# Narrower weights for the low parts of the probabilities in the value products of attention, and another order of their matmuls

## The chip, the cores and the metric

The kernel runs on one core of one Trainium2 chip. The metric is device time in microseconds (us), the median of several runs. Engines are named as the profile names them: PE (TensorE, matmuls) with PEld (its weight loads), DVE (VectorE), ACT (ScalarE), POOL (GpSimd), SP (SyncE, which issues most DMAs).

## The reference

Two layers of a decoder trunk over 1024 tokens of 1024 features, in float32. Each layer has a mixer, two attention branches that run in parallel, and a gated convolutional feed-forward block. What the change touches is the last step of attention, probabilities times values:

```python
p = jnp.exp(scores - mx)                                    # dilated windows, softmax
o = jnp.einsum('brhnqk,brhnkc->brhnqc', p, vw) / den
...
attn = jnp.where(causal, jnp.exp(log_sigmoid(z) + later), 0.0)  # stick-breaking
return jnp.einsum('bhqk,bhkc->bhqc', attn, vt)
```

There are 4 stick-breaking heads, which see all earlier keys, and 12 dilated-window heads in three groups: one near group (each query sees the last 128 keys) and two far groups with dilations 4 and 16. A head has 64 features.

## The kernel before, in words

**Split numbers.** PE takes its operands as fp32r, which holds fewer bits than float32. So an operand x is kept as two parts, hi = x rounded to fp32r (ACT, line 145) and lo = x - hi (DVE, line 153), and a product is a sum of hi x hi, hi x lo and lo x hi. The dense projections spell that out as three matmuls of 512 moving columns (lines 1063 to 1065, and `product`, lines 187 to 189).

**The value product.** Values lie in tiles of 128 keys by 128 columns: columns 0 to 63 are the high half of the head's 64 features, 64 to 127 the low half. Such a tile is the stationary operand (the weight) of a matmul. The moving operand is a block of probabilities, transposed by PE so that keys lie on the partitions, and split by `parts` (line 651) into a high tile and a low tile. Each block of values meets both tiles in two matmuls, which add into one PSUM bank `o`: partitions 0 to 63 collect the products with the high half, 64 to 127 those with the low half. `fold` (line 658) adds the two halves when the bank is complete. So before the change four products are summed: hi x hi, hi x lo, lo x hi and lo x lo.

**Units.** One call of `apply` is called a unit here. Its matmuls have 256 or 128 moving columns, 128 where a block of keys meets only one of two query blocks:

- `stick_item`, `apply` (line 754; profile line 763): one item for each head and each pair of query blocks, 16 items a layer; in each item units for kb = 2qp, 2qp-2, ..., 0, two key blocks each. In the first unit of an item the second key block has 128 columns; otherwise all have 256.
- `near_item`, `apply` (line 822; profile line 830): 4 items a layer, each with five units by the list of `sets` at line 851, for example `[(2, [2, 3]), (3, [3])]`, a pair of 256 columns and a pair of 128; the last unit is `[(7, [7])]` alone.
- `far_item`, `apply` (line 931; profile lines 936 and 938): 16 items a layer, each with two units (one for each far group), of 256 and of 128 columns.

**The order around it.** PE's instruction order is the order of the program. `attend` (line 374) interleaves, in small steps, an item's turns (transposes of probabilities, then `parts`) and its applies, each apply after the next turn, with the scores of the next item. After each such step `dense.advance(rate)` puts in steps of the dense projections for later items: RATE (1.03 to 1.32) for the stick-breaking items, RATE_N (0.75) for near and RATE_T (0.58) for far. With a rate under 1, some steps have no dense work behind them, and then a unit is followed by the next transposes or scores. DMAs for later items are issued from `fetch` by counts of such steps. DVE, ACT and the queues get their order from a planner that knows priorities (`high_priority`) and orders set by hand (`add_manual_dep`).

Of the kernel before, what the change touches and what calls it, by code (L numbers as in the profile page):

```python
# [16 lines left out]
P = 128  # L17
# [23 lines left out]
IN_ORDER = {ET.PE, ET.Activation, ET.DVE, ET.Pool}  # L41
HEAD = 4
SECOND = 0.35
RATE = (1.03, 1.17, 1.27, 1.32)
RATE_N = 0.75
RATE_T = 0.58
# [18 lines left out]
def trunk_kernel(ctx, tc, x, norm1, w_in, b_gate, w_br, w_o, norm2, w_up, conv_w, conv_b, w_down, norm_f, out, depth=None, probe=None):  # L65
    nc = tc.nc
    act, dve, pe, pool = nc.scalar, nc.vector, nc.tensor, nc.gpsimd
# [64 lines left out]
    def small(name, dtype=F32):  # L132
        return sb.tile([P, 512], dtype, tag="pt", bufs=PT, name=name)
# [517 lines left out]
    def parts(src, n, name):  # L651
# [3 lines left out]
            split(hi[:, :n], lo[:, :n], src[:, :n], "is")  # L655
        return hi, lo

    def fold(dst, o):

        n = o.shape[-1]  # L660
        tmp = small("fold")
        with tc.high_priority(offset=AHEAD):
            act.copy(tmp[0:64, :n], o[64:128, :])
            dve.tensor_tensor(dst, o[0:64, :], tmp[0:64, :n], ALU.add)
# [33 lines left out]
    def stick_item(dense, u, qp):  # L698
        q, k, v = R["slots"][:, qp], R["kv"][:, 0, :], R["kv"][:, 1, :]
        pr, s = divmod(u, 2)  # L700
        rows, st, shared, left = {}, {}, {}, []

        def score(a):
            L = P * (2 * qp + a + 1)
            bt = rows[a] = sb.tile([P, T], F32, tag="p4", bufs=4, name="beta")
            if a == 0:
                st[0] = sb.tile([P, 2, T], F32, tag="xa", bufs=4, name="stay")
            sv = st[0][:, a, :]
            for c1 in range(L, 0, -512):
                c0 = max(0, c1 - 512)  # L710
                w = c1 - c0
                z = bank("s", "z")
                scores(z[:, :w], *(q[:, x, a * P : a * P + P] for x in range(2)), k[:, c0:c1])
                with tc.high_priority(offset=AHEAD):
                    act.activation(bt[:, c0:c1], z[:, :w], AF.Sigmoid)
                    last = act.activation(sv[:, c0:c1], z[:, :w], AF.Sigmoid, scale=-1.0)
                    if (u, qp, a, c0) == (3, 0, 1, 0):
                        one = table(AF.Exp, zero[:, 0:1])
                        tc.add_manual_dep(one.ins, last.ins.name, NO_SYNC, reason="behind")
                    if c1 == L:  # L720
                        pool.affine_select(bt[:, L - P : L], bt[:, L - P : L], [[-1, P]], ALU.is_gt, 0.0, base=0, channel_multiplier=1)
                (SCANS if c1 == L else left).append((shared, bt, sv, c0, c1, L))
            if a:
                SCANS.extend(left)
                dense.rows += 1
                scans(2)

        def scans(most):

            while SCANS and most:  # L730
                most -= 1
                _, bt, sv, c0, c1, L = SCANS.pop(0)
                rev = sv[:, c0:c1][:, ::-1]
                if c1 == L:
                    one = dve.tensor_tensor_scan(rev, rev, over[:, HF - (c1 - c0) : HF][:, ::-1], 1.0, ALU.mult, ALU.max)
                else:
                    one = dve.tensor_tensor_scan(rev, rev, zero[:, 0:1].to_broadcast([P, c1 - c0]), sv[:, c1 : c1 + 1], ALU.mult, ALU.add)
                if "dve" in LAST:
                    tc.add_manual_dep(one.ins, LAST["dve"], NO_SYNC, reason="in turn")
                k0, k1 = max(0, c0 - 1), c1 - 1  # L740
                with tc.high_priority(offset=AHEAD):
                    LAST["mult"] = dve.tensor_tensor(bt[:, k0:k1], bt[:, k0:k1], sv[:, k0 + 1 : k1 + 1], ALU.mult).ins.name

        def turn(kb):
            while any(x[0] is shared and x[4] > kb * P for x in SCANS):
                scans(1)
            tp = bank("t", "sb_t")
            todo = [(j, a) for j in range(2) for a in range(2) if kb + j <= 2 * qp + a]
            for c, (j, a) in enumerate(todo):
                pe.transpose(tp[:, c * P : c * P + P], rows[a][:, (kb + j) * P : (kb + j + 1) * P], ident)  # L750
            shared[kb] = parts(tp, len(todo) * P, "sb")
            scans(2)

        def apply(kb):
            first = kb == 2 * qp
            if first:
                shared["o"] = bank("o", "sb_o")[:, :256]
                dense.free[qp] = u + 1
            o = shared["o"]
            for j in range(2):  # L760
                c = P if first and j else 0
                for p in (0, 1):
                    pe.matmul(
                        o[:, c:256],
                        v[:, (kb + j) * P : (kb + j + 1) * P],
                        shared[kb][p][:, 256 * j : 256 * j + 256 - c],
                        start=(first and j == 0 and p == 0),
                        stop=(kb == 0 and j == 1 and p == 1),
                        skip_group_check=True,
                    )  # L770
            if kb == 0:
                out_ = small("ob")[0:64, 0:256]
                fold(out_, o)
                nc.sync.dma_start(obd[64 * s : 64 * s + 64, pr, qp * 256 : (qp + 1) * 256], out_)

        sc = [lambda: score(0), lambda: score(1)]
        return sc, [(lambda kb=kb: turn(kb), lambda kb=kb: apply(kb)) for kb in range(2 * qp, -2, -2)]


    def near_item(dense, pr, s):  # L780
# [6 lines left out]
        k, v = kv[:, 0, :], kv[:, 1, :]  # L787
        got, shared = {}, {}
# [33 lines left out]
        def apply(i, some, n, first, last):  # L822
            if first:
                shared["o"] = bank("o", "o0")
            o = shared["o"]
            w = 0
            for kb, bs in some:
                c0, nb = (bs[0] - 4 * n) * P, len(bs) * P
                for p in (0, 1):
                    pe.matmul(  # L830
                        o[:, c0 : c0 + nb],
                        v[:, kb * P : (kb + 1) * P],
                        shared[i][p][:, w * P : w * P + nb],
                        start=(first and w == 0 and p == 0),
                        stop=(last and kb == some[-1][0] and p == 1),
                        skip_group_check=True,
                    )
                w += len(bs)
            if last:
                fold(on[64 * s : 64 * s + 64, pr, n * HF : (n + 1) * HF], o)  # L840
                if s == 1 and n == 1:
                    tp = bank("o", "st0_t")
                    pe.transpose(tp[0:32, 0:P], st.rearrange("p a s b -> p (a s b)"), ident)
                    row = sb.tile([32, P], F32, tag="pt", bufs=PT, name="st0_r")
                    with tc.high_priority(offset=AHEAD):
                        act.copy(row, tp[0:32, 0:P])
                    nc.sync.dma_start(dn[pr].rearrange("c (b p) -> (c b) p", p=P), row)
# [37 lines left out]
    def far_item(dense, pr, s, r, share):  # L885
        i = 8 * pr + 4 * s + r
# [5 lines left out]
        shared = {}  # L892
# [38 lines left out]
        def apply(g):  # L931
            if r % 2 == 0 and g == 0:
                share["o"] = bank("o", "o1")
            o, oc, vt = share["o"], 256 * (r % 2), R["v", i][:, g]
            for p in (0, 1):
                pe.matmul(o[:, oc : oc + 256], vt[:, 0:P], shared[g][p][:, 0:256], start=(r % 2 == 0 and g == 0 and p == 0), stop=False, skip_group_check=True)
            for p in (0, 1):
                pe.matmul(o[:, oc + P : oc + 256], vt[:, P:256], shared[g][p][:, 256:384], start=False, stop=(r % 2 == 1 and g == 1 and p == 1), skip_group_check=True)
            if g == 1:
                dense.applied = i + 1  # L940
            if r % 2 == 1 and g == 1:
                if R["ot", pr] is None:
                    R["ot", pr] = sb.tile([P, T], F32, tag="ot", name="ot")
                fold(R["ot", pr][64 * s : 64 * s + 64, 512 * (r // 2) : 512 * (r // 2) + 512], o)
                if s == 1 and r == 3:
                    join(dense, pr)
# [389 lines left out]
    def mixer(l, pending):  # L1336
# [43 lines left out]
        for j in range(16):  # L1380
            items.append((f"B{j}", [f"FB{j // 4 * 4 + 3}"], [], RATE[3 - j % 4], lambda j=j: stick_item(dense, j // 4, 3 - j % 4)))
        for v in range(4):
# [530 lines left out]
    def enter(l):  # L1913


        def go(rest, last):
# [9 lines left out]

            drive(norm(0, g1[:, 0, :], "t", raw=True), second(), SECOND, 3)
            x_move(1, True)
# [304 lines left out]
```

## Time and profile before

| | |
|---|---|
| time, median of 3 runs | 2612.03 us (2611.89 to 2614.1) |
| span of the profiled execution (its own time) | 2610.5 us |
| PE matmuls busy | 2600.8 us, 12647 instructions |
| PE weight loads | 2178.5 us, 12647 instructions |
| DVE busy | 2085.6 us |
| ACT busy | 1349.7 us |
| mean granted clock of PE | 1.000 |

The span goes from the first to the last instruction of one profiled execution. A timeline row gives the start, the duration (both in us), the engine, the line, the operation, the tiles it writes and reads, and shapes: `128*128` is the weight, the next pair the moving operand (partitions by columns), or, for a load, the weight. Rows of groups end with the count, the busy time in us and the mean of one in ns. Durations of matmuls are modelled and overlap each other, since matmuls are pipelined; starts are recorded. A weight load is shown as an instruction of its own (PEld).

### The profile page before, as it was taken

How to read it: one execution, taken by the hardware profiler on the slowest of the kernel's cores; microseconds unless marked ns; L12 is line 12 of the kernel's file. 1: busy time of each engine (PE TensorE's matmuls, PEld its weight loads, DVE VectorE, ACT ScalarE, POOL GpSimd, SP SyncE). 2: the span in 40 equal slices, each digit the busy share in tenths (PEclk: the TensorE clock that was granted, in tenths of full speed). 3: DMA queues.
4: the chain of work that ended last, by engine and by line, in shares of the span. 5: the costliest groups of instructions: out<-in, count | busy, mean ns of one | idle time of the engine just before them, and what ended most of it. 6: DMA issues, size and time to landing. Idle time of an engine off the chain costs nothing.

```text
span 2610.5 us, 36058 instructions
## 1 busy us (share of the span) xinstructions
PE 2600.8 (100%) x12647; PEld 2178.5 (83%) x12647; DVE 2085.6 (80%) x3485; ACT 1349.7 (52%) x2521; POOL 105.5 (4%) x145
## 2 busy tenths in 40 slices
PE   9999999999999999999999999999999999999999
PEld 8888888888888888888888888888888888888887
DVE  8877777795988888897677788777869888889965
ACT  6555666574554555422445555656645555544225
POOL 3000000030000000000000000000300000000000
PEclk9999999999999999999999999999999999999999
DMA  7433578873244444688344436788633344446963
GB/s 255 151 120 130 163 208 214 236 245 97 90 145 156 142 167 140 235 328 316 145 143 148 127 129 183 196 231 234 208 100 122 122 163 144 150 165 261 344 239 119
DMA packets 401409, 470.60 MB, mean 180 GB/s; under 512 B 24500, under 2 KB 315980, under 8 KB 399436
## 3 DMA queue, kind: packets, MB, share of 16 engines
q1 hardware_dynamic: 400364, 465.90, 55.2%
q0 software_dynamic: 704, 2.13, 0.4%
q8 instruction: 100, 1.64, 0.3%
q14 instruction: 81, 0.66, 0.1%
q10 hardware_dynamic: 160, 0.27, 0.0%
HBM read 305.59 MB, written 162.63 MB: 179 GB/s over the span
## 4 chain that ended last, share of the span: by engine, by line
PE 98%; DVE 1%; ACT 1%; DMA 0%; issue 0%; POOL 0%; DVEq 0%; ACTq 0%; POOLq 0%
PE u_a L1064 6%; PE u_a L1063 6%; PE u_a L1065 6%; PE d_ps L1827 5%; PE d_ps L1828 5%; PE d_ps L1829 5%; PE i_a L1063 5%; PE i_a L1065 5%; PE i_a L1064 5%; PE u_c L1063 3%; PE u_c L1064 3%; PE u_c L1065 3%; PE i_c L1063 3%; PE i_c L1065 3%; PE i_c L1064 3%; PE o_ps L187 2%
## 5 line engine op out<-in xcount | busy, mean ns | idle before, releaser
L145 ACT CAST w_hi<-up_a 128x512 fp32r<-128x512 f32 x280 | 173.9, 622 | 276.8 <-DVE up_a L1681 120.5
L153 DVE TENSOR_TENSOR w_lo<-up_a,w_hi 128x512 fp32r<-128x512 f32 x280 | 189.4, 688 | 83.5 <-ACT w_hi L145 83.5
L145 ACT CAST w_hi<-in_a 128x512 fp32r<-128x512 f32 x252 | 156.2, 622 | 164.7 <-PE i_c L1064 38.5
L153 DVE TENSOR_TENSOR w_lo<-in_a,w_hi 128x512 fp32r<-128x512 f32 x252 | 172.9, 688 | 73.8 <-ACT w_hi L145 65.7
L1838 DVE TENSOR_TENSOR x<-x,d_ps 128x512 f32<-128x512 f32 x220 | 150.1, 684 | 60.3 <-PE d_ps L1829 57.0
L1064 PE MATMUL u_a<-t_lo,w_hi 128*128 128x512 f32 x320 | 124.6, 389 | 0.0
L1063 PE MATMUL u_a<-t_hi,w_hi 128*128 128x512 f32 x320 | 124.6, 389 | 0.0
L1065 PE MATMUL u_a<-hh,w_lo 128*128 128x512 f32 x320 | 124.5, 389 | 0.0
L1064 PE MATMUL u_a<-hl,w_hi 128*128 128x512 f32 x320 | 124.5, 389 | 0.0
L1065 PE MATMUL u_a<-t_hi,w_lo 128*128 128x512 f32 x320 | 124.5, 389 | 0.0
L1063 PE MATMUL u_a<-hh,w_hi 128*128 128x512 f32 x320 | 124.5, 389 | 0.0
L1827 PE MATMUL d_ps<-gd_in,w_hi 128*128 128x512 f32 x316 | 123.3, 390 | 0.0
L1828 PE MATMUL d_ps<-gd_in,w_hi 128*128 128x512 f32 x316 | 123.1, 389 | 0.0
L1829 PE MATMUL d_ps<-gd_in,w_lo 128*128 128x512 f32 x316 | 123.0, 389 | 0.0
L1063 PE MATMUL i_a<-hh,w_hi 128*128 128x512 f32 x288 | 119.2, 414 | 0.0
L1063 PE MATMUL i_a<-t_hi,w_hi 128*128 128x512 f32 x288 | 118.3, 411 | 0.0
L1065 PE MATMUL i_a<-hh,w_lo 128*128 128x512 f32 x288 | 113.2, 393 | 0.0
L1065 PE MATMUL i_a<-t_hi,w_lo 128*128 128x512 f32 x288 | 113.1, 393 | 0.0
L1064 PE MATMUL i_a<-t_lo,w_hi 128*128 128x512 f32 x288 | 113.0, 392 | 0.0
L1064 PE MATMUL i_a<-hl,w_hi 128*128 128x512 f32 x288 | 112.8, 392 | 0.0
L1827 PE MATMUL d_ps<-gd_in,wd 128*128 128x512 f32 x284 | 111.1, 391 | 0.0
L1829 PE MATMUL d_ps<-gd_in,wd 128*128 128x512 f32 x284 | 110.6, 389 | 0.0
(409 smaller groups left out, 7830.6 us busy)
## 6 DMA issues: line engine op xcount, KB each, us to landing
gd<-g SPq DMA_DIRECT2D x154, 512.0 KB, 3.3
gd_in<-gd SPq DMA_DIRECT2D x154, 512.0 KB, 6.3
up_a<-in_w_up_dram SPq DMA_DIRECT2D x80, 512.0 KB, 5.6
in_a<-in_w_in_dram SPq DMA_DIRECT2D x72, 512.0 KB, 5.5
wd_raw<-in_w_down_dram SPq DMA_DIRECT2D x22, 1024.0 KB, 11.4
gin<-gs SPq DMA_DIRECT2D x32, 512.0 KB, 4.2
w_raw<-in_w_o_dram SPq DMA_DIRECT2D x64, 256.0 KB, 2.8
gs<-u SPq DMA_DIRECT2D x48, 256.0 KB, 2.6
```

The source lines that it names most:

```text
L145: one = act.copy(hi, src)
L153: two = dve.tensor_tensor(lo, src, f32(hi), ALU.subtract)
L187: pe.matmul(o, lh, rh, start=(first and i == 0), stop=False, skip_group_check=share)
L1063: pe.matmul(o, w[0][:, c], rh, start=(first and i == 0), stop=False, skip_group_check=True)
L1064: pe.matmul(o, w[0][:, c], rl, start=False, stop=False, skip_group_check=True)
L1065: pe.matmul(o, w[1][:, c], rh, start=False, stop=(last and i == 3), skip_group_check=True)
L1827: pe.matmul(o, wh[:, c], gh, start=(i == 0 and k in (0, 4, 5)), stop=False, skip_group_check=True)
L1828: pe.matmul(o, wh[:, c], gl, start=False, stop=False, skip_group_check=True)
L1829: pe.matmul(o, wl[:, c], gh, start=False, stop=(i == m - 1), skip_group_check=True)
L1838: dve.tensor_tensor(x, x, o, ALU.add)
```

## The change

A new function `values_on` takes a unit's list of (values, columns of `o`, columns of the probabilities). It first multiplies the high probabilities with all 128 columns of each value block, widest block first. Then it goes through the blocks in the opposite order and multiplies the low probabilities with only the first 66 columns of the values, which write partitions 0 to 65 of `o`. So lo x hi stays, and lo x lo goes, but for the first two of its 64 features. The three `apply` functions call it in place of their own loops; the number of matmuls is the same.

```diff
+LOW = 66
...
+    def values_on(o, todo, part_, first, last):
+
+        todo = sorted(todo, key=lambda x: x[1].start - x[1].stop)
+        for i, (vals, to, at) in enumerate(todo):
+            pe.matmul(o[:, to], vals, part_[0][:, at], start=(first and i == 0), stop=False, skip_group_check=True)
+        for i, (vals, to, at) in reversed(list(enumerate(todo))):
+            pe.matmul(o[0:LOW, to], vals[:, 0:LOW], part_[1][:, at], start=False, stop=(last and i == 0), skip_group_check=True)
...
@@ stick_item, apply @@
-            for j in range(2):
-                c = P if first and j else 0
-                for p in (0, 1):
-                    pe.matmul(
-                        o[:, c:256],
-                        v[:, (kb + j) * P : (kb + j + 1) * P],
-                        shared[kb][p][:, 256 * j : 256 * j + 256 - c],
...
+            values_on(
+                o,
+                [(v[:, (kb + j) * P : (kb + j + 1) * P], slice(P if first and j else 0, 256), slice(256 * j, 256 * j + (P if first and j else 256))) for j in range(2)],
+                shared[kb],
+                first,
+                kb == 0,
+            )
@@ near_item, apply @@
-            w = 0
+            w, todo = 0, []
             for kb, bs in some:
                 c0, nb = (bs[0] - 4 * n) * P, len(bs) * P
-                for p in (0, 1):
-                    pe.matmul(
-                        o[:, c0 : c0 + nb],
-                        v[:, kb * P : (kb + 1) * P],
-                        shared[i][p][:, w * P : w * P + nb],
...
+                todo.append((v[:, kb * P : (kb + 1) * P], slice(c0, c0 + nb), slice(w * P, w * P + nb)))
                 w += len(bs)
+            values_on(o, todo, shared[i], first, last)
@@ far_item, apply @@
-            for p in (0, 1):
-                pe.matmul(o[:, oc : oc + 256], vt[:, 0:P], shared[g][p][:, 0:256], ...)
-            for p in (0, 1):
-                pe.matmul(o[:, oc + P : oc + 256], vt[:, P:256], shared[g][p][:, 256:384], ...)
+            todo = [(vt[:, 0:P], slice(oc, oc + 256), slice(0, 256)), (vt[:, P:256], slice(oc + P, oc + 256), slice(256, 384))]
+            values_on(o, todo, shared[g], r % 2 == 0 and g == 0, r % 2 == 1 and g == 1)
```

More of the change, by code (lines that the diff above doesn't have):

```diff
@@ L759, in apply @@
             o = shared["o"]
-            for j in range(2):
-                c = P if first and j else 0
-                for p in (0, 1):
-                    pe.matmul(
-                        o[:, c:256],
-                        v[:, (kb + j) * P : (kb + j + 1) * P],
-                        shared[kb][p][:, 256 * j : 256 * j + 256 - c],
[L767 to L770, printed above, removed]
+            values_on(
[5 more added lines that the diff above has]
+            )
             if kb == 0:
@@ L825, in apply @@
             o = shared["o"]
-            w = 0
+            w, todo = 0, []
             for kb, bs in some:
                 c0, nb = (bs[0] - 4 * n) * P, len(bs) * P
-                for p in (0, 1):
-                    pe.matmul(
-                        o[:, c0 : c0 + nb],
-                        v[:, kb * P : (kb + 1) * P],
-                        shared[i][p][:, w * P : w * P + nb],
[L834 to L837, printed above, removed]
+                todo.append((v[:, kb * P : (kb + 1) * P], slice(c0, c0 + nb), slice(w * P, w * P + nb)))
                 w += len(bs)
+            values_on(o, todo, shared[i], first, last)
             if last:
@@ L934, in apply @@
             o, oc, vt = share["o"], 256 * (r % 2), R["v", i][:, g]
-            for p in (0, 1):
-                pe.matmul(o[:, oc : oc + 256], vt[:, 0:P], shared[g][p][:, 0:256], start=(r % 2 == 0 and g == 0 and p == 0), stop=False, skip_group_check=True)
-            for p in (0, 1):
-                pe.matmul(o[:, oc + P : oc + 256], vt[:, P:256], shared[g][p][:, 256:384], start=False, stop=(r % 2 == 1 and g == 1 and p == 1), skip_group_check=True)
+            todo = [(vt[:, 0:P], slice(oc, oc + 256), slice(0, 256)), (vt[:, P:256], slice(oc + P, oc + 256), slice(256, 384))]
+            values_on(o, todo, shared[g], r % 2 == 0 and g == 0, r % 2 == 1 and g == 1)
             if g == 1:
```

## The prediction

> **What bounds the kernel now.** I read the head of the page, its chain of waits, a table by stretches, the timeline of TensorE around the changed matmuls, the groups by shape, and last the waits.
>
> ```profile
> span 2610.5 us, 36058 instructions
> ...
> PE 2600.8 (100%) x12647; PEld 2178.5 (83%) x12647; DVE 2085.6 (80%) x3485; ACT 1349.7 (52%) x2521; POOL 105.5 (4%) x145
> ...
> PE 98%; DVE 1%; ACT 1%; DMA 0%; issue 0%; POOL 0%; DVEq 0%; ACTq 0%; POOLq 0%
> ```
>
> TensorE is busy for the whole span and is 98% of the chain that ended last. So what an edit of its stream is worth is read from start to start inside that stream: a matmul's shown duration has a pipelined tail in it, and "busy" hides a matmul that waits for its weights. Three shapes matter: a 512-wide matmul of the projections, and the 256-wide and 128-wide matmuls of the value products ("wide" and "narrow" from here; every weight load before has 128 columns). The timeline of one value product of the stick-breaking branch, TensorE's matmuls, then its weight loads:
>
> ```profile
> 90.73 0.28 PE L763 MATMUL sb_o<-sbh,kv 128*128 128x256 f32 x1
> 90.84 0.28 PE L763 MATMUL sb_o<-sbl,kv 128*128 128x256 f32 x1
> 90.96 0.22 PE L763 MATMUL sb_o<-sbh,kv 128*128 128x128 f32 x1
> 91.02 0.28 PE L763 MATMUL sb_o<-sbl,kv 128*128 128x128 f32 x1
> 91.13 0.45 PE L1063 MATMUL i_a<-hh,w_hi 128*128 128x512 f32 x1
> 91.42 0.39 PE L1064 MATMUL i_a<-hl,w_hi 128*128 128x512 f32 x1
> 91.65 0.39 PE L1065 MATMUL i_a<-hh,w_lo 128*128 128x512 f32 x1
> ```
>
> ```profile
> 90.96 0.19 PEld L763 LDWEIGHTS sb_o<-sbl,kv 128*128 128x128 f32 x1
> 91.07 0.19 PEld L1063 LDWEIGHTS i_a<-hh,w_hi 128*128 128x128 f32 x1
> ```
>
> Each load starts when the matmul before it has started, and runs beside it. A 512-wide matmul takes 0.23 us from start to start (91.42 to 91.65), a wide one 0.11 to 0.12, a narrow one 0.06 (90.96 to 91.02). Loads follow each other every 0.11 us (90.96, 91.07). So a load hides behind a 512-wide matmul, just hides behind a wide one, and does not hide behind a narrow one: half of it sticks out. The narrow low product lasts 0.28 where the narrow high one lasts 0.22, and the next 512-wide one 0.45 where the usual is 0.39. These are the two places where a load sticks out, one behind each narrow matmul.
>
> **What a load costs by its columns.** Eight matmuls of one moving column show the pace of loads alone, and two groups of transposes have loads of 32 and of 128 columns:
>
> ```profile
> 673.13 0.97 PEld L538 LDWEIGHTS nrm_t<-ones,nrm 128*128 128x128 f32 x8 [0.35 <-issue]
> ```
>
> ```profile
> L763 PEld LDWEIGHTS sb_o<-sbl,kv 128*128 128x128 f32 x160 | 30.3, 190 | 3.2
> L1034 PEld LDWEIGHTS j_ps<-ident,fx 128*128 128x128 f32 x32 | 3.7, 141 | 0.5
> L843 PEld LDWEIGHTS st_t<-ident,st 128*32 128x32 f32 x4 | 0.4, 94 | 0.0
> ```
>
> (0.97 - 0.19)/7 = 0.111 us a load, so of the 0.19 shown some 0.078 is a latency that the next load doesn't wait for. Take the same latency from the loads of transposes: 141 - 78 = 63 ns for 128 columns and 94 - 78 = 16 ns for 32, or 0.49 and 0.50 ns a column. The pace is proportional to the columns there, with nothing fixed. If the loads of the values behave so, 66 columns take 111 x 66/128 = 57 ns, and show as some 78 + 57 = 135 ns. The bounds: 111 ns (columns don't matter) and 111 - 62 x 0.49 = 81 ns (the columns count only as in a transpose). I take 57, because the two transposes leave no fixed part; 81 and 111 are rivals below.
>
> **The change part by part.** No instruction is added or removed: 360 high and 360 low products stay. The lows load 66 columns instead of 128, and the order of a unit goes from high, low, high, low to high wide, high narrow, low narrow, low wide.
>
> ```profile
> L763 PE MATMUL sb_o<-sbl,kv 128*128 128x256 f32 x128 | 34.1, 283 | 0.0
> L936 PE MATMUL o<-p1l,slots 128*128 128x256 f32 x64 | 18.7, 292 | 0.3 <-DVE p1l L153 0.2
> L938 PE MATMUL o<-p1l,slots 128*128 128x128 f32 x64 | 17.7, 277 | 0.0
> L938 PE MATMUL o<-p1h,slots 128*128 128x128 f32 x64 | 14.3, 223 | 0.0
> L830 PE MATMUL o<-p0l,kv 128*128 128x256 f32 x48 | 13.2, 289 | 0.0
> L763 PE MATMUL sb_o<-sbl,kv 128*128 128x128 f32 x32 | 8.9, 279 | 0.0
> L763 PE MATMUL sb_o<-sbh,kv 128*128 128x128 f32 x32 | 7.2, 224 | 0.0
> L830 PE MATMUL o<-p0l,kv 128*128 128x128 f32 x24 | 6.6, 277 | 0.0
> L830 PE MATMUL o<-p0h,kv 128*128 128x128 f32 x24 | 5.3, 222 | 0.0
> ```
>
> Narrow lows: 32 + 64 + 24 = 120. Eight of them stand alone (the last key block of each of the 8 near items, [(7,[7])]); 112 share a unit with a wide pair. Wide lows: 128 + 64 + 48 = 240; less 112 leaves 128, that is 64 units of two wide pairs.
>
> First exposure, the narrow low waiting for its own load. In the new order that load has 57 ns and runs behind the narrow high (60 ns): hidden. The price is the difference of the low and the high group: 279 - 224 = 55, 277 - 223 = 54, 277 - 222 = 55. So 32 x 55 + 64 x 54 + 24 x 55 = **6.5 us**.
>
> Second exposure, what follows the narrow low. Now a load of 66 columns (the low wide's) lies behind the narrow low, and the full load of whatever follows the unit lies behind the low wide, which covers it as 90.73 to 90.96 do. Before a 512-wide matmul the price is 0.06 (0.45 against 0.39); I take 55 ns, as for the first. Before a transpose it is smaller:
>
> ```profile
> 442.44 0.30 PE L926 MATMUL t<-ident,p 128*128 128x128 f32 x1
> 442.57 0.27 PE L927 MATMUL t<-ident,p 128*128 128x128 f32 x1
> ...
> 1814.97 0.29 PE L926 MATMUL t<-ident,p 128*128 128x128 f32 x1
> ```
>
> 0.02 to 0.03, taken as 25 ns. In the timeline 32 of the 112 units are followed by transposes (the far ones between these two rows); the other 80 by a dense matmul or, where the narrow pair came first, by their own wide pair at 0.05. So 80 x 55 + 32 x 25 = **5.2 us**. The eight lone ones keep this exposure, since their low is followed by the dense stream as before.
>
> Units of two wide pairs:
>
> ```profile
> 96.00 0.28 PE L763 MATMUL sb_o<-sbh,kv 128*128 128x256 f32 x1
> 96.11 0.28 PE L763 MATMUL sb_o<-sbl,kv 128*128 128x256 f32 x1
> 96.23 0.40 PE L1063 MATMUL i_a<-t_hi,w_hi 128*128 128x512 f32 x1
> ```
>
> 0.12 a matmul where 0.11 is the least (90.73 to 90.84): two of the four loads shrink, at 5 ns each, 64 x 10 ns = **0.6 us**; bounds 0 and 64 x 20 = 1.3.
>
> The order itself. The low of a unit waits for VectorE's subtraction, and a high no longer stands behind it:
>
> ```profile
> 422.73 0.28 PE L936 MATMUL o<-p1h,slots 128*128 128x256 f32 x1
> 423.08 0.38 PE L936 MATMUL o<-p1l,slots 128*128 128x256 f32 x1
> ...
> PEld o L936 <- DVE p1l L153: 1.7, 5, 0.4
> ```
>
> Here the low starts 0.35 after the high instead of 0.12. Five such waits, 1.7 us together, could lose at most the narrow high that now fills them, 5 x 0.06 = 0.3 us, and half a load each. I book 0; at the other end, with waits that grow as TensorE comes earlier, I allow -1 us. The queues of SyncE, ScalarE and GpSimd get the same instructions; the fold still waits for the unit's last matmul, which comes earlier.
>
> Sum: 6.5 + 5.2 + 0.6 = 12.3 us. The profiled span of 2610.5 becomes 2598.2. The median shown, 2612.03, lies 1.5 above that span, and what lies around the span does not change: **2599.7 us**.
>
> What must keep up is the far stage, where units are densest:
>
> ```profile
> 420.00:531.00 111.00, 110.93 (x655) 96.25 (x654) 81.84 (x188) 70.34 (x161) 2.72 (x6) 1.00 0.88 234
> ```
>
> Columns after the length: TensorE, loads, VectorE, ScalarE, GpSimd, granted clock, DMA share. VectorE has 26% free and the DMA engines 12%; the 64 far units give about 64 x 55 + 36 x 55 + 28 x 25 = 6.2 us, 3.1 a layer, 2.8% of 111. That fits, narrowly for DMA.
>
> **Rivals.**
>
> *The load doesn't shrink with its columns, or only partly.* With 111 ns the narrow high hides 57, the low narrow waits 54, the low wide waits 54 behind it: the two exposures only move inside the unit, gain 0, **2612**. For it: all loads of fp32r shown have 128 columns. Against it: 94 against 141 ns. With 81 ns each stays exposed by 81 - 57 = 24: 12.3 - (2 x 112 + 8) x 0.024 = 6.7 gained, **2605.3**.
>
> *The far stage gives nothing,* because the transfers that feed it are the limit once TensorE is faster: 12.3 - 6.2 = 6.1 gained, **2605.9**. For it:
>
> ```profile
> DMA to landing us min/median/max: 2.5/4.7/8.2
> ```
>
> for the key and query tile, of which one is consumed about every 6.7 us, and a DMA share of 0.88. Against it: no wait of TensorE for that tile stands among its waits.
>
> *Slower: the array is set up anew for a smaller weight.* Each unit goes from 128 columns to 66 and back. If each switch emptied the array, it would cost about the pipelined tail of a matmul, 389 - 227 = 0.16 us as the shown 0.39 less the 0.23 from start to start. 184 units x 2 x 0.16 = 59 lost against 12 gained, **2659**; it decides from 12.3/368 = 33 ns a switch on. Against it stands a matmul after a 32-column weight beside one after a 128-column transpose:
>
> ```profile
> 372.00 0.48 PE L1063 MATMUL i_a<-t_hi,w_hi 128*128 128x512 f32 x1
> ...
> 348.97 0.48 PE L1063 MATMUL i_c<-hh,w_hi 128*128 128x512 f32 x1
> ```
>
> The first follows the 32-column st_t (line 843), the second a 128-column transpose (line 818): the same 0.48, so that switch costs nothing that shows. The Trainium skill says in "TensorEngine Tiling (Array Packing)", Key Properties, that a change of tiling mode drains TensorE; by that rule this rival would hold if 66 columns were another mode than 128, and the two rows above do not bear it out.
>
> *More: loads don't overlap at all.* Then every low, not only those behind narrow ones, saves 62 x 0.87 = 54 ns: 360 x 54 = 19.4, **2592.6**. The Trainium skill has such a rule in "TensorE: Matmul & The Clock Gate", Part 3, The mechanism: a load overlaps a running matmul only where their row groups differ. The trace disagrees: here loads and matmuls both use all 128 rows, and 0.23 from start to start has no room for 0.11 of load beside 512 columns when 256 columns take 0.11.
>
> **How the numbers follow.** Forecast 0.72; partly shrinking load or far stage without gain (about 2605.5) 0.13; no gain (2612) 0.07; slower 0.05; no overlap 0.03. About 0.2%, 5.2 us, is what a measurement can tell from no change: faster means below 2606.8. Most of the 0.13 counts as faster (0.11): faster 0.72 + 0.11 + 0.03 = 0.86, same 0.02 + 0.07 = 0.09, slower 0.05. The forecast's own range is 2596 to 2603 (0.6 to 1.3 for wide units, waits of -1 to +0.3, 25 to 55 ns as the price before dense matmuls, other engines' orders shifted by some us). Taking in the rivals near 2605.5 it is 2594 to 2608, which leaves out the two of no gain and slower, 0.12, and part of no overlap.
>
> **What would show it.** Low loads at about 135 ns instead of 190. Narrow lows at 223 ns, like the narrow highs, instead of 277. The 512-wide matmul after a unit at 0.39 instead of 0.45, and from a mixed unit's first matmul to the second 512-wide one behind it 0.58 instead of 0.69 (90.73 to 91.42). High loads unchanged. Wrong would be: loads of 66 columns at 190 ns; narrow lows still at 277 and wide lows at 330 (no gain); new waits of z on t_kq in the far stage; or a gap of over 33 ns where a 66-column matmul follows a full one.

## The result, and the profile after

The changed kernel takes 2602.55 us (median of 5 runs, 2601.4 to 2603.86) against 2612.03 us (2611.22 to 2614.1, 5 runs): a ratio of 0.9964, 95% interval 0.9952 to 0.9975. That is 9.5 us faster; forecast were 2599.7 us, 12.3 us faster. The profiled execution took 2603.86 us, the longest of the five, with a span of 2602.2 us, 8.3 less than before.

The head of the page of the changed kernel, and its chain:

```profile
span 2602.2 us, 36060 instructions
...
PE 2589.6 (100%) x12647; PEld 2165.4 (83%) x12647; DVE 2084.7 (80%) x3485; ACT 1349.5 (52%) x2521; POOL 105.6 (4%) x145
...
PE 93%; DVE 3%; ACT 2%; DMA 1%; issue 1%; SPq 0%; POOL 0%; DVEq 0%; ACTq 0%
```

The engines' counts are the same and TensorE is still busy throughout, but it now holds 93% of the chain where it held 98%. That is a hint of waits and no more, since the order alone (below), which gains nothing, shows 96%. The timeline of the unit that the prediction showed; `x2` joins a wide and a narrow matmul of one line:

```profile
90.20 0.34 PE L663 MATMUL sb_o<-sbh,kv 128*128 128x256 f32 x2
90.38 0.34 PE L665 MATMUL sb_o<-sbl,kv 128*66 128x128 f32 x2
90.56 0.39 PE L1059 MATMUL i_a<-hh,w_hi 128*128 128x512 f32 x1
90.79 0.39 PE L1060 MATMUL i_a<-hl,w_hi 128*128 128x512 f32 x1
```

From the unit's first matmul to the second 512-wide one behind it are 0.59 us (90.20 to 90.79), 0.69 before, and that 512-wide one shows 0.39 instead of 0.45. The groups by shape, loads first, then narrow lows (line 665) beside narrow highs (line 663):

```profile
L665 PEld LDWEIGHTS sb_o<-sbl,kv 128*66 128x66 f32 x160 | 18.5, 136 | 0.0
...
L665 PE MATMUL o<-p1l,slots 128*66 128x128 f32 x64 | 14.8, 231 | 1.2 <-DVE p1l L154 0.7
L663 PE MATMUL o<-p1h,slots 128*128 128x128 f32 x64 | 14.2, 222 | 0.0
...
L663 PE MATMUL sb_o<-sbh,kv 128*128 128x128 f32 x32 | 7.1, 223 | 0.0
L665 PE MATMUL sb_o<-sbl,kv 128*66 128x128 f32 x32 | 7.1, 222 | 0.0
```

A load of 66 columns shows 136 ns (135 forecast), and a narrow low lasts as long as a narrow high, but for the far items, where it waits for VectorE.

Both programs multiply in the same order outside the units, and the instructions of ScalarE, VectorE, GpSimd and SyncE stand in the same order in both traces. So their starts can be compared one by one. I took, for each unit, the time from the matmul before it to the third one behind it, in both. Mixed units before a dense matmul or before scores are shorter by 102 to 114 ns (medians by kind), the 20 before transposes by 74 to 77, lone narrow pairs by 20 to 59, most wide units by 14. Each kind's median times its count gives 12.5 us. But a handful of far units is longer, so that all units together are only 9.0 us shorter, and what lies between the units is 0.8 us longer, most of it small waits in the output projection behind the attention (o_ps for x and hl). 9.0 - 0.8 = 8.2 us, within 0.1 of the difference of the spans. The longer units:

| start before, us | after against before, us | median of its kind |
|---|---|---|
| 516.05 and 1805.51, last but one of each far stage | +0.36, +0.39 | -0.10 |
| 529.10 and 1818.55, last of each far stage | +0.37, +0.40 | -0.10 |
| 1771.80 | +1.24 | -0.10 |

The four in the upper rows cost 1.5 us, and 0.4 us of gain that they should have had. The fifth is a matter of one execution: in ten of the twelve other profiles below it was 0.4 to 0.5 shorter than before, and in none longer by more than 0.04. The 0.8 us between the units can't be called gain handed back: the order alone, which gains nothing, has the same two waits in the output projection (0.9 and 0.6 us). What brings them stays open. The waits of weight loads, changed kernel (total us, times, longest):

```profile
PEld o L663 <- ACT p1h L146: 2.4, 3, 1.4
PEld o L665 <- DVE p1l L154: 2.2, 7, 0.5
```

Of the first, 1.4 us are the fifth unit; the other two are the units at 516 and 1806 us, 0.5 each. Before, there was only the second, with 1.7 us in five waits.

### The profile page after: what moved, and what is told of

The parts are those of the page before. It is cut to its first block, busy times and chain, and to the rows that moved or that the text cites. A ratio compares the mean times of both kernels' runs of the same rounds, so it can differ in the third digit from the quotient of the medians.

```text
span 2602.2 us, 36060 instructions
## 1 busy us (share of the span) xinstructions
PE 2589.6 (100%) x12647; PEld 2165.4 (83%) x12647; DVE 2084.7 (80%) x3485; ACT 1349.5 (52%) x2521; POOL 105.6 (4%) x145
## 4 chain that ended last, share of the span: by engine, by line
PE 93%; DVE 3%; ACT 2%; DMA 1%; issue 1%; SPq 0%; POOL 0%; DVEq 0%; ACTq 0%
PE u_a L1060 6%; PE u_a L1061 6%; PE u_a L1059 6%; PE d_ps L1823 5%; PE d_ps L1825 5%; PE d_ps L1824 5%; PE i_a L1059 5%; PE i_a L1060 5%; PE i_a L1061 5%; PE u_c L1059 3%; PE u_c L1060 3%; PE u_c L1061 3%; PE i_c L1059 2%; PE i_c L1061 2%; PE i_c L1060 2%; PE o_ps L188 2%
```

## The experiments

Each run is timed beside the kernel before, whose medians in these sessions were 2612.1 to 2612.7 us.

**Columns alone.**

```diff
-        todo = sorted(todo, key=lambda x: x[1].start - x[1].stop)
         for i, (vals, to, at) in enumerate(todo):
             pe.matmul(o[:, to], vals, part_[0][:, at], ...)
-        for i, (vals, to, at) in reversed(list(enumerate(todo))):
-            pe.matmul(o[0:LOW, to], vals[:, 0:LOW], part_[1][:, at], ...)
+            pe.matmul(o[0:LOW, to], vals[:, 0:LOW], part_[1][:, at], ...)
```

> Columns alone: the lows load 66 columns, but the order stays high, low, high, low. Theory (a load costs 0.87 ns a column and sticks out behind a 128-wide matmul): the narrow low no longer waits for its own load, but the full load of whatever follows it still sticks out. In the trace narrow lows at 223 ns instead of 277, and the 512-wide matmul after a mixed unit still at 0.45 us. Inside the units 6.5 us, and 0.6 from the wide lows; of 12.3 us inside the units the whole change kept 8 to 9.5, so some 5 to 6.5 us faster than before, 2605.5 to 2607. Rival (the order is only decoration): as the whole change, 2602.5. Rival (the gain is all from the order): 2612.

Measured 2606.92 us against 2612.68, ratio 0.9978 (0.9969 to 0.9987): 5.8 us. The groups and the timeline of the unit shown above:

```profile
L663 PE MATMUL o<-p1l,slots 128*66 128x128 f32 x64 | 14.3, 224 | 0.0
L663 PE MATMUL sb_o<-sbl,kv 128*66 128x128 f32 x32 | 7.2, 224 | 0.0
```

```profile
89.86 0.45 PE L1057 MATMUL i_a<-hh,w_hi 128*128 128x512 f32 x1
90.14 0.40 PE L1058 MATMUL i_a<-hl,w_hi 128*128 128x512 f32 x1
```

The narrow low no longer waits (224), while the full load behind it still sticks out (0.45): the first exposure is won by the columns alone, the second needs the order too.

**Order alone.**

```diff
-LOW = 66
+LOW = 128
```

> Order alone: high products first, low ones in the opposite order, but the lows keep all 128 columns (the product of the low parts with each other stays too). Theory: the two loads that stick out move inside the unit, to the narrow low (277 ns or more) and to the wide low behind it (about 0.33 us instead of 0.28); gain 0 inside the units, 2610 to 2613. Rival (the order matters because the lows have more time to arrive): 1 to 3 us faster. Rival (the gain is all from the order): 2602.5.

Measured 2611.38 us, ratio 0.9995 (0.9986 to 1.0003): no difference. The exposed loads have moved, as expected. Low and high wide products of the far items, then the narrow low:

```profile
L665 PE MATMUL o<-p1l,slots 128*128 128x256 f32 x64 | 21.3, 333 | 0.0
L663 PE MATMUL o<-p1h,slots 128*128 128x256 f32 x64 | 19.4, 303 | 0.0
L665 PE MATMUL o<-p1l,slots 128*128 128x128 f32 x64 | 17.9, 279 | 0.0
```

The narrow low still has 279, and the wide low behind it has 333. So the order by itself is worth nothing that can be measured, yet with narrow weights it is worth 9.5 - 5.8 = 3.7 us. The rival that lows get more time to arrive is not ruled out by a median that is 1.3 us lower and inside the interval. The trace shows a little of it: the loads wait 0.3 us in all for p1l where they waited 1.7, and the units at 516 and 1806 us are 0.23 shorter each.

**64 columns.** `LOW = 64`.

> As the whole change but 64 columns in place of 66, so no product of low with low is left. Theory: 64 columns load in 56 ns in place of 57, nothing else changes: 2602.5 within 1 us. Rival (64 columns and fewer put the array in another mode, and each change of mode empties it): from 33 ns a change on it loses all that was gained; with the 0.16 us of a matmul's tail it is near 2660.

Measured 2604.05 us against 2612.68, ratio 0.9967 (0.9955 to 0.9979), the same as the whole change within the intervals. A load shows 134 ns. A drained array at each switch is excluded: even 33 ns a switch would have taken the whole gain, and mixed units before dense matmuls or scores are 101 to 108 ns shorter than before the change, much as with 66 columns. This bears on the rule of the Trainium skill in "TensorEngine Tiling (Array Packing)", Key Properties, that a change of tiling mode drains TensorE: with 64 and 128 columns by turns in fp32r no drain shows here. Whether 64 columns are another mode for this type, no run tells.

**96 columns.** `LOW = 96`.

> As the whole change but 96 columns in place of 66 (the product of low with low is left for 32 of the 64 features). Theory (proportional): a load of 96 columns costs 83 ns and is shown as about 161; behind a narrow matmul of 57 to 60 it sticks out by about 24, twice in each of 112 units and once in 8: 5.6 us of the 12.3 are lost, 6.7 are left inside the units, about 4 to 5.5 in the time: 2606.5 to 2608. Rival (any weight narrower than 128 columns is cheap): 2602.5. Rival (the load is paid in halves of the array, up to 64 or up to 128 columns, 66 being hidden only by luck): loads of 190 ns, 2612.

Measured 2607.24 us, ratio 0.9980 (0.9972 to 0.9989): 5.4 us. Loads, and the narrow low:

```profile
L665 PEld LDWEIGHTS sb_o<-sbl,kv 128*96 128x96 f32 x160 | 21.3, 162 | 0.0
...
L665 PE MATMUL sb_o<-sbl,kv 128*96 128x128 f32 x32 | 7.9, 247 | 0.0
```

162 ns where 161 was expected, and 247 - 223 = 24 ns stick out. With 134 at 64 columns, 136 at 66 and 190 at 128, the load is a straight line: 56/64 = 0.87 ns a column upon some 78. The Trainium skill has a load's time as columns/1.2 ns in "TensorE: Matmul & The Clock Gate", section LDWEIGHTS, 0.83 ns a column, and the pace here, 0.87, agrees within 5%; the transposes' loads of the prediction, at 0.49, don't fit it.

**Where the missing 3 us went: stages apart.** First the change in the stick-breaking and near items alone (`far_item.apply` as before), then in the far items alone.

```diff
-            todo = [(vt[:, 0:P], slice(oc, oc + 256), slice(0, 256)), (vt[:, P:256], ...)]
-            values_on(o, todo, shared[g], ...)
+            for p in (0, 1):
+                pe.matmul(o[:, oc : oc + 256], vt[:, 0:P], shared[g][p][:, 0:256], ...)
+            for p in (0, 1):
+                pe.matmul(o[:, oc + P : oc + 256], vt[:, P:256], shared[g][p][:, 256:384], ...)
```

> The change in the stick-breaking and near items alone; the far items multiply as before. Theory (what was lost on the way was lost in the far stage, whose last units wait for ScalarE and VectorE, and the rest is kept): 48 mixed units and 64 wide ones gain 6.3 us inside the units (3.9 stick-breaking and 2.4 near in the trace of the whole change) and keep it: 2605.5 to 2607 against 2612.3, and the four far units that wait for their low part wait no longer than before. Rival (a quarter is lost everywhere alike): 4.8 us, 2607.5 or more.

Measured 2606.21 us against 2612.10, ratio 0.9978 (0.9969 to 0.9987): 5.9 us of the 6.3 inside the units.

The far items alone are the inverse edit.

> The change in the far items alone. Theory: 36 x 0.106 + 28 x 0.076 = 5.9 us inside the 64 far units, of which the last two units before the end of the far stage of each layer give back about 0.45 each, 2 us in all, because ScalarE and VectorE do not come earlier; 3 to 4.5 us faster, 2608 to 2609.5. In the trace the units at 516, 529, 1806 and 1819 us of the time before are 0.3 us or more longer than before. Rival (lost everywhere alike): 4.5, 2608, and no single unit longer. Rival (the units wait because TensorE is ahead by what the earlier stages gained): no unit is longer, 5.9, 2606.5.

Measured 2609.56 us, ratio 0.9989 (0.9981 to 0.9998): 2.5 us of 5.9. The units at 516, 529, 1806 and 1819 us are longer by 0.38, 0.37, 0.40 and 0.38, as in the whole change. So the loss is made inside the far stage, and TensorE need not come into it early.

**What the last far units wait for.** One suspect was the cast of the stick-breaking outputs, which stands ahead of the last unit's parts:

```diff
-        dense.hooks = [lambda: in_two("b", [0]), lambda: branch_in(0)]
+        dense.hooks = [None, lambda: branch_in(0)]
         dense.finish()
+        in_two("b", [0])
         in_two("b", [1])
```

> The whole change, and the first half of the cast of the stick-breaking outputs (in_two of b) is issued after the dense work is finished instead of when its last group begins. Theory: this cast (two of 0.58 on ScalarE, two of 0.65 on VectorE) stands ahead of the last far unit's parts and makes its low part late by 0.35 to 0.75 us a layer; moved, this wait goes, up to 1 us faster than the whole change (2601.5 to 2602.5), unless the branch products then wait for the cast (up to 2 us slower). Rival (the wait is from the unit's own chain, scores to exponent to transpose): the low part stays late by 0.3 us or more.

Measured 2603.70 us, ratio 0.9966 (0.9953 to 0.9978), and the last units are still 0.33 and 0.37 longer than before. But the run does not test the suspect. In its trace the instructions of TensorE, VectorE, ScalarE and GpSimd stand in the same order as with the whole change, and the cast is still right ahead of the last unit's low part: on VectorE `ol_b` starts at 522.91 us and `p1l` at 524.11, where the whole change has 521.93 and 523.14. The planner put it back where it was.

Another was the row of factors, whose buffer a later cast of probabilities takes over:

```diff
-            row = sb.tile([32, P], F32, tag="pt", bufs=PT, name="f_r")
+            row = sb.tile([32, P], F32, tag="sw", bufs=1, name="f_r")
```

> The whole change, and the 32 x 128 row of factors on its way to DRAM (f_r) lies in another buffer, so that no cast of probabilities waits for its DMA to land (6 to 7.7 us). Theory: the one unit of layer 2 that waited 1.1 us for p1h after that DMA no longer waits in any profile, 0 to 1.3 us faster than the whole change by how late the DMA lands: 2601.3 to 2602.5. Rival (that wait comes from ScalarE's own work): the unit still waits, 2602.5.

Measured 2602.42 us, ratio 0.9962 (0.9949 to 0.9976): nothing against 2602.55. ScalarE no longer waits for that DMA before `p1h` (3.1 us in two waits with the whole change), so the change does what it should. The unit at 1771.8 no longer waits in this profile, but it also didn't in eight others without it: what the DMA costs differs from one execution to the next. The four units are still 0.35 to 0.71 longer than before.

The third suspect came out of VectorE's stretches. The columns after the length are TensorE, loads, VectorE, ScalarE, GpSimd; before the change, and after it:

```profile
1786.00:1796.00 10.00, 10.00 (x62) 8.87 (x62) 9.58 (x18) 2.86 (x8) 0.00 (x0) 1.00 0.64 182
```

```profile
1777.00:1787.00 10.00, 10.00 (x65) 8.87 (x64) 9.58 (x17) 3.21 (x8) 0.00 (x0) 1.00 0.75 201
```

VectorE is 96% busy over 10 us, before the change as after it, where the whole far stage had 74%. The timeline after the change shows with what, and what is late next, up to the last unit but one:

```profile
1784.74 2.11 DVE L1014 TENSOR_TENSOR on<-on,fx 128x512 f32<-128x512 f32 x2
...
1794.34 0.62 ACT L146 CAST w_hi<-in_a 128x512 fp32r<-128x512 f32 x1 [1.54 <-DVE in_a L1194]
...
1796.08 0.46 ACT L146 CAST p1h<-t 128x384 fp32r<-128x384 f32 x1
...
1796.57 0.56 DVE L154 TENSOR_TENSOR p1l<-t,p1h 128x384 fp32r<-128x384 f32 x1 [0.70 <-ACT p1h L146]
1796.59 0.30 PEld L663 LDWEIGHTS o<-p1h,slots 128*128 128x128 f32 x2 [0.51 <-ACT p1h L146]
...
1797.18 0.19 PEld L665 LDWEIGHTS o<-p1l,slots 128*66 128x66 f32 x2 [0.29 <-DVE p1l L154]
```

The join of the first half's outputs (`on` with the factors `fx`) lies in the middle of the far stage, and the ten us that end with it are VectorE's fullest. What it can't gain there it doesn't make up later: from the join (1793.29 before, 1784.74 after) to the end of the stage VectorE's and ScalarE's instructions come 8.5 to 8.6 us earlier than before. ScalarE can't be earlier by itself, since its `w_hi` waits for VectorE's `in_a`, and `p1h` comes behind that. TensorE is 9.1 us ahead in the unit before the last but one (1803.37 to 1794.27), so it has to wait for the next probabilities. In the last unit the low part stands behind the cast of the stick-breaking outputs as well:

```profile
1808.27 1.28 DVE L154 TENSOR_TENSOR ol_b<-ob_in,oh_b 128x512 fp32r<-128x512 f32 x2
...
1809.48 0.55 DVE L154 TENSOR_TENSOR p1l<-t,p1h 128x384 fp32r<-128x384 f32 x1
...
1810.08 0.20 PEld L665 LDWEIGHTS o<-p1l,slots 128*66 128x66 f32 x2 [0.49 <-DVE p1l L154]
```

To test what VectorE's load does, steps of the join went to GpSimd:

```diff
+                eng = pool if step in (1, 2) else dve
...
-                    one = dve.tensor_tensor(mine, mine, first[...], ALU.mult)
+                    one = eng.tensor_tensor(mine, mine, first[...], ALU.mult)
...
-                    one = dve.tensor_tensor(mine, mine, far, ALU.add)
-                tc.add_manual_dep(one.ins, LAST["dve"], NO_SYNC, reason="in turn")
+                    one = eng.tensor_tensor(mine, mine, far, ALU.add)
+                if eng is dve:
+                    tc.add_manual_dep(one.ins, LAST["dve"], NO_SYNC, reason="in turn")
```

> The whole change, and the second and third step of the first join (four products and sums onto `on`, 1.05 to 1.10 us each, 4.3 us a layer on VectorE between 1777 and 1787 us) run on GpSimd, which is idle there. Theory (VectorE works without a gap in the last 20 us of the far stage, and the units there wait for it, so TensorE's gain is not kept): the far units at 516, 529, 1806 and 1819 us of the time before no longer lose 0.3 to 0.7, nor the narrow gain that they should have; up to 2 us faster than the whole change, 2600.5 to 2602. Rival (they wait for ScalarE or for the transposes): these units stay late, 2602.5. Rival (GpSimd's products are late for the second join, or slow VectorE down): 2603.5 or more.

Measured 2616.26 us, ratio 1.0012 (1.0003 to 1.0022): 13.7 us slower than the whole change. The four units are indeed not late (-0.35, 0.00, -0.33, +0.03 against before), but two others each lose 6.3 us. VectorE waits for the steps on GpSimd:

```profile
489.48 0.42 DVE L916 CUSTOM_DVE_ANT_1 p<-z,bias 128x256 f32<-128x256 f32 x1 [6.79 <-POOL on L1013]
```

With the second step on GpSimd the planner gives the buffer of its factors to the next tile of probabilities, and GpSimd has to wait for the factors' DMA first (5.8 us in layer 1). Since TensorE then stands still for 6 us, this run can't show that VectorE's load was the cause.

The same edit in the kernel before, and all three steps with the row in its own buffer, met the same wait:

> The kernel before, and the same two steps on GpSimd; no value product is changed. Theory: TensorE was slower by 2 to 3 us at that place and met VectorE's late parts in few units (1.7 us of waits in all), so there is less to win: 0 to 1 us, 2611 to 2612.3. Rival (VectorE held up TensorE there before too): as much as with the change, 2 us, 2610.

Measured 2625.80 us, ratio 1.0050 (1.0038 to 1.0063), 13.6 us slower than before. It says nothing on the theory.

> The whole change, all three steps of the first join on GpSimd (5.7 us a layer off VectorE), and the row of factors in its own buffer. Theory: as the run with two steps, and the one cast that waits for the row's DMA doesn't: 2600 to 2601.5. Rival (the first step frees the buffer that the second half's folds write, and GpSimd is late with it): a wait at the first fold of the second half, 2602 or more.

Measured 2615.87 us, ratio 1.0014 (1.0005 to 1.0023), with 6.0 and 7.0 us lost in the same two units.

The third step alone (`step in (2,)`) leaves that buffer as it was, and VectorE's other instructions in their order:

> The whole change, and only the third step of the first join (two sums onto `on`, 2.1 us a layer, at 1785 us in the trace of the whole change) on GpSimd; VectorE's other instructions stand in the same order, and no tile of probabilities is refilled late, since the next one that takes this buffer comes some 14 instructions later. Theory (VectorE runs without a gap at the end of the far stage and the last units wait for it): the units at 516 and 1806 us of the time before, 0.35 to 0.41 longer with the whole change, become shorter than before, those at 529 and 1819 by less; 1 to 2 us faster than the whole change, 2600.5 to 2602. Rival (these units wait for ScalarE's casts or their own chain): they stay 0.3 us longer, 2602.5 to 2604. Rival (GpSimd's sums, 1.5 us each, hold up VectorE or a buffer as the runs with two and three steps showed): 2606 or more.

Measured 2600.39 us (2599.68 to 2601.59) against 2612.13, ratio 0.9956 (0.9942 to 0.9969): 11.7 us faster than before and the fastest of all, although its interval overlaps that of the whole change (0.9952 to 0.9975). In its trace the four units are at -0.35, 0.00, -0.33 and +0.02 us against before (the first and third gain more than the usual 0.10, since they waited some 0.25 for their low part before the change too), and all units together gain 12.7 us where the whole change gained 9.0. Of these 3.7 us, 2.2 are the four units, as much as the two times differ, and 1.3 the fifth, which says nothing. VectorE at the join, and the waits of weight loads for the probabilities:

```profile
1775.00:1785.00 10.00, 10.00 (x65) 8.87 (x64) 8.89 (x17) 3.19 (x8) 3.78 (x2) 1.00 0.71 187
```

```profile
PEld o L665 <- DVE p1l L154: 0.6, 3, 0.3
```

2.1 us a layer off VectorE took the waits for low parts from 2.2 to 0.6 us, and the waits for high parts left the list. VectorE's other instructions, and ScalarE's, stand in the same order, but the low part of the last unit but one now comes 11.8 us earlier than before (1805.13 to 1793.31), and TensorE, 11.2 us ahead in the unit before it, no longer waits. So VectorE's backlog from the join was what held the last unit but one of each layer, and made most of the wait in the last. There 0.1 us of the usual gain is still missing; the cast ahead of it, which no run moved, may be the rest.

## Why the prediction was right, and where it was short

- *Loads by columns.* Right: 57 ns of pace and 135 shown were forecast, 136 shown, and 64 and 96 columns lie on the same line. The two rivals of a load that doesn't shrink, or only as in a transpose, fall with that.
- *First exposure, 6.5 us.* Right: the columns alone win it, narrow lows at 222 to 224, and 5.8 us in the time, that of the wide units included.
- *Second exposure, 5.2 us.* Right in size and cause: 74 to 77 ns shorter before transposes and 103 to 114 before dense matmuls, where 55 + 25 and 55 + 55 were forecast; it takes columns and order together. One count was off: of the 32 units put down as followed by transposes, 12 far ones are followed by scores (`z<-t_kq`) and are shorter by 102, some 0.3 us more.
- *Wide units, 0.6 us.* 14 ns each instead of 10: 0.9 us. Inside the units the whole forecast of 12.3 us thus met 12.5.
- *The order itself, 0 us.* Right: with all 128 columns it measures no difference.
- *"That fits" for the far stage.* This is the step that failed. VectorE's free 26% was an average over 111 us. In the ten us that end with the join it had 4%, which the trace before the change already shows; so VectorE could not follow TensorE there, and the last two units of each layer took back 1.5 us and 0.4 of their own gain. Only DMA was named as narrow; VectorE was passed over. The allowance of -1 us for waits that grow was about half of that.
- *Nothing lost behind the attention* was assumed without a word. The profile has 0.8 us more there, in waits of the output projection; as the order alone has them too, they are not explained, and no run took them apart.
- *Rivals.* Far stage without gain: half true, with VectorE in the place of DMA; the far items alone kept 2.5 us of 5.9. Array set up anew: no, at 64 columns either. No overlap of loads: no, wide units won 14 ns and not 2 x 54. The time of 9.5 us leaves 2.8 of the 12.3. The four units show 1.9 of it, and the run with the third step on GpSimd bears that out; that the 0.8 in the output projection would fill the rest is not shown, with runs of one kernel that lie 2 us apart.

## What to carry to other kernels

Read what a weight load costs from start to start, not from busy time: here it was free behind a matmul of 512 columns and half of it was paid behind one of 128, and a narrower weight pays only if the short matmul is followed by that narrow load, so columns and order belong together. Ask of each engine that feeds the faster one how busy it is in the ten microseconds where it is busiest, since an average over the stage says little of a stretch. Moving a line of the program tests an order only if the trace shows the engine's order changed. Work moved to an idle engine takes its buffers along: look at who refills them before the time that it saves.

## What was not expected of the hardware

The same sum of two 128x512 tiles, with a strided view, took 1.08 to 1.10 us on VectorE (whole change) and 1.5 to 2.2 us on GpSimd (two steps or the third alone there), so that the idle engine was a gain only where nothing waited for it.
